# An encoder step on one core: three of the seven products of the FFN's block are accumulated in PSUM onto others

## The chip, the cores and the metric

One core of one Trainium2 chip runs the whole program in one launch. The metric is the device time of one execution in microseconds; the median of the runs shown counts. The core's engines are TensorE (PE, with its weight loader PEld), VectorE (DVE), ScalarE (ACT), GpSimd (POOL) and SyncE (SP, which issues DMAs). Each runs its own queue in order and waits on semaphores for the others.

## The reference

One inference step of an encoder with two layers (DEPTH = 2) and model width 1024, for 512 prompt tokens and 8 x 16 sample tokens. Each layer mixes the tokens by four parallel branches (a gated convolution, two kinds of attention, pooling), and then applies a gated feed-forward network:

```python
h2 = _rmsnorm(x, g_norm[l, 2])
gu = h2 @ w_ffn_in[l]
f = (jax.nn.silu(gu[..., :D_FF]) * gu[..., D_FF:]) @ w_ffn_out[l]
x = x + _rmsnorm(f, g_norm[l, 3])
```

D_FF is 2816. The change lies in the second and third of these lines, in the product with w_ffn_in and what follows it.

## The kernel before

All 640 tokens are treated as one matrix with the model width on the partitions. A product in fp32 is made of three passes: a weight block w is split into a high part whi (a rounded copy, made by ACT at L117) and the rest wlo (a subtraction, by DVE at L274), the tokens likewise into h2's high and low part, and PE adds w-high x x-high, w-high x x-low and w-low x x-high in PSUM.

The FFN's first product is tiled by j = 0 to 21, each j standing for 128 gate and 128 up channels. The first three j (J0 = 3) are done directly. The other 19 are done in `strassen(j)` by a seven-product scheme (Winograd's form of Strassen's): the 1024 x 256 weights of a j are cut into four blocks (upper and lower half of the model width, gate and up), the tokens' matrix into four quadrants (upper and lower half of the width, first and last 320 tokens). Seven products of 512-deep sums replace eight; the price is sums of weight blocks (`weight_sums`, four GpSimd instructions per j, issued for j + 1 in the middle of block j), sums of token quadrants (`token_sums`, made once per layer while the direct j run), and sums of the products.

One product is the function `product(ps, j, p)`: four slices of depth, three passes each, twelve matmuls of 128 x 320 into one PSUM bank. `moving[p]` is the token operand, and `w_sub` hands out the weight block p, split two products ahead. After the second slice, `flush` issues the subtractions wlo that are pending, so that DVE's queue holds, per product, one wlo and then the additions that read the product.

Before the change the seven products of a j go to seven banks: the first to a bank of the pool O, the next two to S, then T, two of D, and S again. The pools hold two D tiles (each of two halves, [128, 2, 512] in fp32), two S, one T and one O, eight banks in all. The order of the products is 0 to 6 in `moving`'s count, and set by `range(7)` in the list of weight chunks. With the products called by Winograd's numbers (p1, p6, p7, p5, p2, p4, p3 in that order), ACT copies p1 to s1, and DVE forms u2 = p6 + s1, u3 = p7 + u2, c22 = p5 + u3, u2 = p5 + u2, s1 = p2 + s1, s1 = u3 - p4, u2 = p3 + u2: seven additions of 128 x 320, each of which reads one bank. ACT applies Silu to s1 (L1868) and, in the next block, to u2 (L1878); DVE multiplies act by s1 and by c22 (L1849, L1881).

All instructions stand in the order in which the code is written; nothing reorders them. In SBUF the results act, X and Y come from a list of 33 slots.

Of the kernel before, what the change touches and what calls it, by code (L numbers as in the profile page):

```python
# [11 lines left out]
AF = mybir.ActivationFunctionType  # L12
ALU = mybir.AluOpType
# [12 lines left out]
HT = T // 2  # L26
# [11 lines left out]
J0 = 3  # L38
GATE_F = 3
GATE_STEP = 0.8  # L40
FO_ORDER = (4, 0, 1, 2, 3, 5, 6, 7, 8, 9, 10)
EPS = 1e-6

# [17 lines left out]
def encoder_step(ctx: ExitStack, tc: tile.TileContext, I, O):  # L61
    nc = tc.nc
    V, A, G, PE, SP = nc.vector, nc.scalar, nc.gpsimd, nc.tensor, nc.sync
# [37 lines left out]
    def psD():  # L101
        return psd.tile([128, 2, 512], F32, tag="D", name=nm("D"))

    def psS():
        return pss.tile([128, 512], F32, tag="S", name=nm("S"))

    def psT():
        return pst.tile([128, 512], F32, tag="T", name=nm("T"))

    def psO():  # L110
        return pso.tile([128, 512], F32, tag="O", name=nm("O"))
# [4 lines left out]
    def copy(out, in_, scale=1.0):  # L116
        A.activation(out=out, in_=in_, func=AF.Copy, scale=scale)  # L117
# [83 lines left out]
    chunks = []  # L201
    for l in range(L):
        for c in ORDER:
            if c == "v":
                chunks += [((k, l, i), I["w_v"][l, g, i], 1032, "n") for g, k in enumerate(("vd", "vf")) for i in range(2)]
            else:
                chunks.append((("in", l, c), I["w_in"][l, c], 1024, "n"))
        for ph, bs in enumerate(PHASES):
            if ph == 2:
                for p in range(5):  # L210
                    for part, f in (((0,), 2 * p - 2), ((1, 2), 2 * p - 1), ((3, 4, 5, 6), -1)):
                        if p < 4:
                            chunks.append((("gs", l, p), None, part, "s"))
                        if f >= 0:
                            chunks.append((("b", l, 2, f), I["w_branch"][l, 1, f, :, 256:512], 256, "n"))
                continue
            for f in range(9):
                for b in bs if f < 8 else bs[:1]:
                    if f < 8:
                        chunks.append((("g", l, ph, b, f), I["w_gate"][l, min(ph, 1), b, f], 1024, "n"))  # L220
                    if b == bs[0] and f > 0:
                        n = 256 * len(bs)
                        chunks.append((("b", l, ph, f - 1), I["w_branch"][l, min(ph, 1), f - 1, :, 256 * bs[0]:256 * bs[0] + n], n, "n"))
        for h, c in ((0, 0), (0, 1), (1, 0), (0, 2), (1, 1), (1, 2), (0, 3), (1, 3)):
            chunks.append((("o", l, h, c), I["w_out"][l, h, c], 1024, "nx"[h]))
        for j in range(NJ):
            if j < J0 or j % 2 == 0:
                for g in range(2):
                    chunks.append((("fi", l, j, g), I["w_fi"][l, j, g], 1024, "n" if j < J0 else "r"))
            if j >= J0:  # L230
                chunks.append((("fs", l, j), None, range(7), "s"))
        for c in FO_ORDER:
            chunks.append((("fo", l, 0, c), I["w_fo"][l, 0, c], 1024, "n"))
        for c in (0, 1, 2, 3, 7, 4, 8, 5, 9, 6, 10):
            chunks.append((("fo", l, 1, c), I["w_fo"][l, 1, c], 1024, "x" if c >= 7 else "n"))
# [172 lines left out]
    def v2(t):  # L408
        return t.rearrange("p (a b) -> p a b", a=2)
# [50 lines left out]
    def quadrant(h, r, c):  # L460
        return [[x[:, 4 * r + k, c * HT:(c + 1) * HT] for k in range(4)] for x in h]

    def token_sums(h, dst, at, step=0.6):
        hv = [f32(x) for x in h]

        def quad(x, r, c, q):
            return hv[x][:, 4 * r + 2 * q:4 * r + 2 * q + 2, c * HT:(c + 1) * HT]

        def chain(E, out, first, terms, q):
            o = v2(out)  # L470
            for n, (x, r, c, op) in enumerate(terms):
                a = o if n else quad(0, *first, q) if isinstance(first, tuple) else v2(first)
                E.tensor_tensor(out=o, in0=a, in1=quad(x, r, c, q), op=op)  # L473

        t = {}
        P_, M_ = ALU.add, ALU.subtract

        def form0(q):
            t[q] = [alloc() for _ in range(4)]
            chain(V, t[q][0], (0, 1), ((0, 0, 0, M_), (1, 0, 1, P_), (1, 0, 0, M_)), q)  # L480
            chain(G, t[q][2], (1, 1), ((0, 0, 1, M_), (1, 1, 1, P_), (1, 0, 1, M_)), q)

        def form1(q):
            o = v2(t[q][1])
            V.tensor_tensor(out=o, in0=quad(0, 1, 1, q), in1=v2(t[q][0]), op=M_)
            V.tensor_tensor(out=o, in0=o, in1=quad(1, 1, 1, q), op=P_)

        def form3(q):
            chain(V, t[q][3], t[q][1], ((0, 1, 0, M_), (1, 1, 0, M_)), q)
            t["formed"] = q  # L490

        def hi(i, q):
            copy(dst(i, q)()[0], t[q][i])

        def lo(i, q):
            d = dst(i, q)()
            sub(d[1], t[q][i], f32(d[0]))
            free(t[q][i])
            t["done"] = t.get("done", 0) + 1

        for q in range(2):
            for fn in (form0, form1, form3):
                after(at, lambda fn=fn, q=q: fn(q))
                at += 2.5 * step
            for i in (1, 0, 2, 3):
                if dst(i, q):
                    after(at, lambda i=i, q=q: hi(i, q))
                    after(at + step, lambda i=i, q=q: lo(i, q))
                    at += step
        return t  # L510
# [490 lines left out]
    def layer(l, Htag, Otag, hT, first_units):  # L1001
# [750 lines left out]
        h2 = (big(Otag + "h"), big(Otag + "l"))  # L1752

        def lhs_o(k, t):
            return tuple(m[:, t * 128:(t + 1) * 128] for m in S.merged[k])

        start = mix_phase(8, lhs_o, "o", range(8), (), range(8), 1, xsrc[2 * l], xsrc[2 * l + 1],
                          {"first": (("fi", l, 0, 0), ("fi", l, 0, 1)), "g": (l, 2), "hi": h2[0], "lo": h2[1]}, lambda n: need(lambda: len(S.merged) > n))
# [50 lines left out]
        tq = (big(Htag + "h"), big(Htag + "l"))  # L1809
        load_blocks(J0)  # L1810
        start(lambda i, Dt: ev_fi(0, i, Dt))
        token_sums(h2, lambda i, q: lambda: [x[:, 2 * i + q, :] for x in tq], 0.0, 0.54)
        for j in range(1, J0):
            for g in range(2):
                Dt = psD()
# [12 lines left out]
        moving = [quadrant(h2, 0, 0), t_op(1), t_op(2), t_op(0), quadrant(h2, 1, 0), t_op(3), quadrant(h2, 1, 1)]  # L1828
        tail = []

        def product(ps, j, p):
            wh, wl = w_sub(("fs", l, j), p)
            xh, xl = moving[p]
            for k in range(4):
                a, b = wh[:, k * 128:(k + 1) * 128], wl[:, k * 128:(k + 1) * 128]
                for pi, (w, x) in enumerate(((a, xh), (a, xl), (b, xh))):
                    PE.matmul(ps[:, :HT], w, x[k], start=(k == 0 and pi == 0), stop=(k == 3 and pi == 2))  # L1837
                if k == 1:
                    flush()
                    tick(1.0)  # L1840
            return ps[:, :HT]

        def strassen(j):
            act, X, Y = alloc(), alloc(), alloc()
            acts[j] = act
            s1, u2, u3, c22 = X[:, :HT], X[:, HT:], Y[:, :HT], Y[:, HT:]

            def add(out, a, b, op=ALU.add):
                V.tensor_tensor(out=out, in0=a, in1=b, op=op)  # L1849

            p1 = product(psO(), j, 0)
            for fn in tail[:1]:
                fn()
            copy(s1, p1)
            p6 = product(psS(), j, 1)
            for fn in tail[1:]:
                fn()
            tail.clear()
            add(u2, p6, s1)
            p7 = product(psS(), j, 2)  # L1860
            add(u3, p7, u2)
            sums(j + 1)
            p5 = product(psT(), j, 3)
            add(c22, p5, u3)
            add(u2, p5, u2)
            p2 = product(psD()[:, 0, :], j, 4)
            add(s1, p2, s1)
            A.activation(out=act[:, :HT], in_=s1, func=AF.Silu)  # L1868
            p4 = product(psD()[:, 0, :], j, 5)
            if j == NJ - 1:  # L1870
                convert(0)
            add(s1, u3, p4, ALU.subtract)
            add(act[:, :HT], act[:, :HT], s1, ALU.mult)
            p3 = product(psS(), j, 6)
            add(u2, p3, u2)

            def gate():
                A.activation(out=act[:, HT:], in_=u2, func=AF.Silu)  # L1878

            def last():  # L1880
                V.tensor_tensor(out=act[:, HT:], in0=act[:, HT:], in1=c22, op=ALU.mult)  # L1881
                free(X, Y)

            tail.extend((gate, last))
# [46 lines left out]
        start = mix_phase(22, lhs_f, "fo", fo_order, range(7), range(14, 22), 3, xsrc[2 * l + 1], O["y"] if last else xsrc[2 * l + 2], nxt, lambda n: convert(n + 1))  # L1931
# [183 lines left out]
```

## Time and profile before

| What | Value |
|---|---|
| Time, median of 3 runs | 2123.02 us (2122.63 to 2124.85) |
| Span of the profiled execution | 2121.1 us |
| Time over that span | 1.9 us, from the median |
| PE busy | 2044.4 us, 96% of the span |
| DVE busy | 1489.7 us, 70% |
| ACT busy | 983.7 us, 46% |
| POOL busy | 694.6 us, 33% |

The times come from runs of their own. The span of the profiled execution reaches from its first to its last instruction; it is the profile's own time, and the durations in the rows below are of that execution. Busy time is an average over stages with different limits, so a stage is read by itself: with the view that sums each engine's busy time in a stretch, and with the waits of that stretch. In a timeline row the first number is the start and the second the duration, in us; what stands in brackets is the engine's idle time before it and what ended it.

### The profile page before, as it was taken

To read this page: it belongs to the slowest core of one execution; us is meant where nothing else is said; L and a number is where in the kernel's file an instruction comes from. 1 tells how busy PE (TensorE), PEld (TensorE's weight loads), DVE (VectorE), ACT (ScalarE), POOL (GpSimd) and SP (SyncE) were. 2 spreads that over 40 slices of the span, in tenths; PEclk is the share of its full clock that TensorE was granted. 3 is DMA by queue.
4 is the path that set the end of the run, shared out by engine and by line. 5 is a ranking of instruction groups with operands and counts; after the bars stand their busy time and mean duration, and the time that the engine had idled before them with its cause. 6 is when DMAs were issued, how large, how long until landed. Compare 5 with 4: busy or idle time off the path is not lost.

```text
span 2121.1 us, 34713 instructions
## 1 busy us (share of the span) xinstructions
PE 2044.4 (96%) x13050; PEld 1927.9 (91%) x13050; DVE 1489.7 (70%) x2746; ACT 983.7 (46%) x2100; POOL 694.6 (33%) x618
## 2 busy tenths in 40 slices
PE   7999999989999999999999999999899999999998
PEld 7999999988889999988899999999888899999887
DVE  5677477689768888853475774775996698888432
ACT  5556455545443433443356554565444444334431
POOL 3111055465315444400040101554751345543000
PEclk9999999999999999999999999999999999999999
DMA  4312244332251222222523122443223422222223
GB/s 146 108 61 86 72 145 138 124 123 75 94 172 60 80 81 91 89 80 75 169 75 117 57 82 82 152 149 130 83 72 115 159 75 80 80 88 67 92 97 119
DMA packets 100744, 214.35 MB, mean 101 GB/s; under 512 B 10896, under 2 KB 35056, under 8 KB 100576
## 3 DMA queue, kind: packets, MB, share of 16 engines
q1 hardware_dynamic: 99552, 209.16, 29.6%
q0 software_dynamic: 1024, 2.98, 0.4%
q8 instruction: 102, 1.67, 0.3%
q14 instruction: 66, 0.54, 0.1%
HBM read 196.02 MB, written 16.08 MB: 100 GB/s over the span
## 4 chain that ended last, share of the span: by engine, by line
PE 68%; DVE 18%; issue 6%; ACT 3%; DMA 2%; POOL 2%; SPq 0%; DVEq 0%; ACTq 0%; POOLq 0%
PE D L376 21%; PE D L1632 11%; PE S L1837 7%; DVE wlo L274 6%; PE D L1837 4%; PE O L1632 3%; PE T L1632 3%; PE D L1413 2%; DVE s L1849 2%; PE T L1837 2%; PE O L1837 2%; PE D L1274 2%; DVE s L473 1%; PE O L808 1%; ACT whi L117 1%
## 5 line engine op out<-in xcount | busy, mean ns | idle before, releaser
L274 DVE TENSOR_TENSOR wlo<-raw,whi 128x512 fp32r<-128x512 f32 (+2 forms) x388 | 294.6, 764 | 183.1 <-ACT whi L117 178.7
L117 ACT ACTIVATE whi<-raw 128x512 fp32r<-128x512 f32 (+2 forms) x390 | 230.3, 606 | 166.9 <-issue 73.8
L274 DVE TENSOR_TENSOR wlo<-s,whi 128x512 fp32r<-128x512 f32 x196 | 210.7, 1077 | 17.9 <-ACT whi L117 16.6
L117 ACT ACTIVATE s<-s 128x512 fp32r<-128x512 f32 (+7 forms) x294 | 176.3, 619 | 91.7 <-POOL s L1425 38.7
L376 PE MATMUL D<-Qh,whi 128*128 128x320 f32 (+2 forms) x736 | 177.1, 315 | 4.0 <-DVE s L1417 3.6
L376 PE MATMUL D<-Ph,whi 128*128 128x320 f32 (+2 forms) x736 | 176.8, 314 | 4.2 <-DVE s L1417 3.5
L338 POOL TENSOR_TENSOR r<-ms,mhalf 128x1 f32<-128x1 f32 x40 | 22.0, 551 | 477.1 <-DVE ms L1677 408.5
L376 PE MATMUL D<-Qh,wlo 128*128 128x320 f32 (+2 forms) x736 | 174.3, 311 | 3.8 <-DVE wlo L274 3.8
L376 PE MATMUL D<-Ph,wlo 128*128 128x320 f32 (+2 forms) x736 | 173.8, 310 | 4.3 <-DVE wlo L274 4.3
L376 PE MATMUL D<-Ql,whi 128*128 128x320 f32 (+2 forms) x736 | 173.8, 310 | 0.0
L376 PE MATMUL D<-Pl,whi 128*128 128x320 f32 (+2 forms) x736 | 173.4, 310 | 0.0
L746 POOL TENSOR_TENSOR s<-s,s 128x512 fp32r<-128x512 f32 x64 | 85.0, 1328 | 181.9 <-ACT s L117 168.9
L117 ACT ACTIVATE whi<-s 128x512 fp32r<-128x512 f32 x196 | 117.3, 621 | 36.4 <-PE S L1837 12.4
L758 POOL TENSOR_TENSOR s<-s,s 128x512 fp32r<-128x512 f32 x64 | 92.9, 1469 | 123.0 <-ACT s L117 100.9
L376 PEld LDWEIGHTS D<-Qh,whi 128*128 128x128 f32 x736 | 123.5, 190 | 6.8 <-DVE s L1417 4.4
L376 PEld LDWEIGHTS D<-Qh,wlo 128*128 128x128 f32 x736 | 125.2, 189 | 4.6 <-DVE wlo L274 4.6
L376 PEld LDWEIGHTS D<-Ph,wlo 128*128 128x128 f32 x736 | 124.5, 189 | 5.3 <-DVE wlo L274 5.3
L376 PEld LDWEIGHTS D<-Ph,whi 128*128 128x128 f32 x736 | 123.0, 189 | 7.0 <-DVE s L1417 4.0
L376 PEld LDWEIGHTS D<-Ql,whi 128*128 128x128 f32 x736 | 125.6, 189 | 0.2
L376 PEld LDWEIGHTS D<-Pl,whi 128*128 128x128 f32 x736 | 125.1, 189 | 0.6 <-DVE Pl L120 0.4
L451 POOL TENSOR_TENSOR s<-V,V 128x512 f32<-128x512 f32 x48 | 77.1, 1607 | 94.4 <-DMA V<-in_w_fi 67.0
L117 ACT ACTIVATE s<-T 128x320 fp32r<-128x320 f32 (+6 forms) x132 | 50.9, 386 | 99.1 <-PE T L520 61.5
(487 smaller groups left out, 5978.9 us busy)
## 6 DMA issues: line engine op xcount, KB each, us to landing
raw<-in_w_gate SPq DMA_DIRECT2D x48, 512.0 KB, 3.5
raw<-in_w_fi SPq DMA_DIRECT2D x48, 512.0 KB, 3.5
raw<-in_w_fo SPq DMA_DIRECT2D x44, 512.0 KB, 3.5
V<-in_w_fi SPq DMA_DIRECT2D x80, 256.0 KB, 3.0
raw<-in_w_in SPq DMA_DIRECT2D x32, 512.0 KB, 3.4
s<-in_ck_d SPq DMA_DIRECT2D x32, 256.0 KB, 4.3
s<-in_cv_d SPq DMA_DIRECT2D x32, 256.0 KB, 4.0
s<-in_ck_f SPq DMA_DIRECT2D x32, 256.0 KB, 4.1
```

Source lines behind the costliest of these rows:

```text
L117: A.activation(out=out, in_=in_, func=AF.Copy, scale=scale)
L274: E.tensor_tensor(out=lo, in0=raw, in1=hi, op=ALU.subtract)
L338: G.tensor_tensor(out=out, in0=ssum, in1=mhalf[:, :n], op=ALU.pow)
L376: PE.matmul(Dt[:, h, :c1 - c0], a, b[:, k, c0:c1], start=(start and pi == 0), stop=(stop and pi == 2))
L451: G.tensor_tensor(out=o[:, :512], in0=x, in1=y, op=op)
L746: G.tensor_tensor(out=lo[:, :512], in0=raw[:, :512], in1=f32(hi[:, :512]), op=ALU.subtract)
L758: G.tensor_tensor(out=lo[:, :512], in0=t[:, :512], in1=f32(hi[:, :512]), op=ALU.subtract)
L1274: PE.matmul(acc[t], x, w[:, kk, :], start=(k == 0 and pi == 0), stop=(k == 7 and pi == 2))
L1413: PE.matmul(Dt[:, h, :HT], w[:, b, k, :], x[:, 2 * br + k, h * HT:(h + 1) * HT], start=(c == 0), stop=(c == 5))
L1632: PE.matmul(ps, a, b, start=(first and pi == 0), stop=(last and pi == 2))
L1837: PE.matmul(ps[:, :HT], w, x[k], start=(k == 0 and pi == 0), stop=(k == 3 and pi == 2))
L1849: V.tensor_tensor(out=out, in0=a, in1=b, op=op)
```

## The change

The three products p2, p7 and p4 no longer get banks of their own: p2 is accumulated onto p1, p7 onto p6, p4 onto p6 + p7, and p3 onto p5. A block uses one S tile (`pa`, for p1 and p2) and one D tile, whose first half (`pb`) holds p6, p7 and p4 and whose second half (`pd`) holds p5 and p3. The order of the products becomes p1, p6, p2, p7, p5, p4, p3 (FS_ORDER). So that p4 may be added, the fourth token sum is formed with the other sign (`negate`). DVE adds five times from PSUM per block: u2 = pb + s1, u3 = pb + s1, c22 = pd + u3, s1 = pb + s1, u2 = pd + u2. The first Silu reads `pa` directly.

```diff
+FS_ORDER = (0, 1, 4, 2, 3, 5, 6)
...
-                chunks.append((("fs", l, j), None, range(7), "s"))
+                chunks.append((("fs", l, j), None, FS_ORDER, "s"))
...
         def form3(q):
-            chain(V, t[q][3], t[q][1], ((0, 1, 0, M_), (1, 1, 0, M_)), q)
+            if negate:
+                o = v2(t[q][3])
+                V.tensor_tensor(out=o, in0=quad(0, 1, 0, q), in1=v2(t[q][1]), op=M_)
+                V.tensor_tensor(out=o, in0=o, in1=quad(1, 1, 0, q), op=P_)
+            else:
+                chain(V, t[q][3], t[q][1], ((0, 1, 0, M_), (1, 1, 0, M_)), q)
...
-        def product(ps, j, p):
+        def product(ps, j, p, more=False):
...
-                    PE.matmul(ps[:, :HT], w, x[k], start=(k == 0 and pi == 0), stop=(k == 3 and pi == 2))
+                    PE.matmul(ps, w, x[k], start=(not more and k == 0 and pi == 0), stop=(k == 3 and pi == 2), skip_group_check=more)
...
-            p1 = product(psO(), j, 0)
+            pa, pbd = psS()[:, :HT], psD()
+            pb, pd = pbd[:, 0, :HT], pbd[:, 1, :HT]
...
+            product(pa, j, 0)
             for fn in tail[:1]:
                 fn()
-            copy(s1, p1)
-            p6 = product(psS(), j, 1)
+            copy(s1, pa)
+            product(pb, j, 1)
             for fn in tail[1:]:
                 fn()
             tail.clear()
-            add(u2, p6, s1)
-            p7 = product(psS(), j, 2)
-            add(u3, p7, u2)
+            add(u2, pb, s1)
+            product(pa, j, 4, True)
+            A.activation(out=act[:, :HT], in_=pa, func=AF.Silu)
             sums(j + 1)
-            p5 = product(psT(), j, 3)
-            add(c22, p5, u3)
-            add(u2, p5, u2)
-            p2 = product(psD()[:, 0, :], j, 4)
-            add(s1, p2, s1)
-            A.activation(out=act[:, :HT], in_=s1, func=AF.Silu)
-            p4 = product(psD()[:, 0, :], j, 5)
+            product(pb, j, 2, True)
+            add(u3, pb, s1)
+            product(pd, j, 3)
+            add(c22, pd, u3)
+            product(pb, j, 5, True)
             if j == NJ - 1:
                 convert(0)
-            add(s1, u3, p4, ALU.subtract)
-            add(act[:, :HT], act[:, :HT], s1, ALU.mult)
-            p3 = product(psS(), j, 6)
-            add(u2, p3, u2)
+            add(s1, pb, s1)
+            V.tensor_tensor(out=act[:, :HT], in0=act[:, :HT], in1=s1, op=ALU.mult)
+            product(pd, j, 6, True)
+            add(u2, pd, u2)
```

How this stands in the queues is shown at two places, both in one block of layer 0. The first is PE's queue, before the change: the matmuls with which the products in places 1 to 5 of a block open, and the third matmul of each, which is the first to use wlo. S, T and D are PSUM tiles, Ph, Pl, Qh and Ql the high and low parts of the tokens, whi and wlo those of the weights; what stands in brackets are the engines' semaphores that the row waits for.

```order
L1837 MATMUL S_8461<-Ph_7540,whi_8422 128x320 [waits Activation_49]
...
L1837 MATMUL S_8461<-Ph_7540,wlo_8423 128x320 [waits DVE_49]
...
L1837 MATMUL S_8480<-Ph_7540,whi_8443 128x320 [waits DVE_49,Activation_49]
...
L1837 MATMUL S_8480<-Ph_7540,wlo_8444 128x320 [waits DVE_49]
...
L1837 MATMUL T_8506<-Ph_7540,whi_8462 128x320 [waits Activation_49]
...
L1837 MATMUL T_8506<-Ph_7540,wlo_8463 128x320 [waits DVE_49]
...
L1837 MATMUL D_8529<-Qh_7011,whi_8481 128x320 [waits Activation_49]
...
L1837 MATMUL D_8529<-Qh_7011,wlo_8482 128x320 [waits DVE_49]
```

The same queue with the change: the opening matmuls of the products in places 2 to 6 and of the next block's first, with the third matmul of places 2 and 4.

```order
L1843 MATMUL S_8421<-Qh_7011,whi_8423 128x320 [waits Activation_49]
...
L1843 MATMUL S_8421<-Qh_7011,wlo_8424 128x320 [waits DVE_49]
...
L1843 MATMUL D_8422<-Ph_7540,whi_8441 128x320 [waits DVE_49,Activation_49]
...
L1843 MATMUL D_8422<-Ph_7540,whi_8459 128x320 [waits DVE_49,Activation_49]
L1843 MATMUL D_8422<-Pl_7541,whi_8459 128x320
L1843 MATMUL D_8422<-Ph_7540,wlo_8460 128x320
...
L1843 MATMUL D_8422<-Ph_7540,whi_8484 128x320 [waits DVE_49,Activation_49]
...
L1843 MATMUL D_8422<-Qh_7011,whi_8505 128x320 [waits DVE_49,Activation_49]
...
L1843 MATMUL S_8560<-Qh_7011,whi_8522 128x320 [waits Activation_49]
```

The wait for DVE has moved from the third matmul to the first in places 3 to 6, and the third no longer has one. The second place is DVE's queue in the same block with the change, from the addition u2 on (s_8419 holds s1 and u2, s_8420 holds u3 and c22, s_8418 is act).

```order
L1856 TENSOR_TENSOR s_8419<-D_8422,s_8419 128x320 [waits PE_49]
L275 TENSOR_TENSOR wlo_8460<-s_8333,whi_8459 128x512 [waits Activation_49]
L275 TENSOR_TENSOR wlo_8485<-raw_8214,whi_8484 128x512 [waits DMAHW6_49,DVE_49,Activation_49]
L1856 TENSOR_TENSOR s_8420<-D_8422,s_8419 128x320 [waits PE_49]
L275 TENSOR_TENSOR wlo_8506<-s_8336,whi_8505 128x512 [waits Activation_49]
L1856 TENSOR_TENSOR s_8420<-D_8422,s_8420 128x320 [waits DVE_49,PE_49]
L275 TENSOR_TENSOR wlo_8523<-V_8351,whi_8522 128x512 [waits DMAHW7_49,Activation_49]
L1856 TENSOR_TENSOR s_8419<-D_8422,s_8419 128x320 [waits PE_49]
L1878 TENSOR_TENSOR s_8418<-s_8418,s_8419 128x320 [waits DVE_49]
L275 TENSOR_TENSOR wlo_8541<-s_8477,whi_8540 128x512 [waits Activation_49]
L1856 TENSOR_TENSOR s_8419<-D_8422,s_8419 128x320 [waits PE_49]
```

All five additions now read the one D tile of the block, one after each of places 1, 3, 4, 5 and 6. The queues of SP and POOL hold the same instructions in the same order as before.

## Rows read from the trace of the kernel before

**Rows 1.** The page, its head and the engines' busy time.
```profile
span 2121.1 us, 34713 instructions
...
PE 2044.4 (96%) x13050; PEld 1927.9 (91%) x13050; DVE 1489.7 (70%) x2746; ACT 983.7 (46%) x2100; POOL 694.6 (33%) x618
```

**Rows 2.** Busy us of PE, PEld, DVE, ACT, POOL; PEclk: both seven-product stages.
```profile
673.25:913.32 240.07, 236.89 (x1599) 233.82 (x1597) 207.69 (x302) 97.61 (x189) 111.65 (x71) 1.00 0.23 79
1722.44:1961.92 239.48, 236.52 (x1598) 233.93 (x1597) 207.12 (x302) 97.57 (x189) 113.05 (x72) 1.00 0.24 79
```

**Rows 3.** Timeline of PE: first matmuls of two neighbouring blocks.
```profile
749.00 0.31 PE L1837 MATMUL O<-Qh,whi 128*128 128x320 f32 x1
...
761.30 0.31 PE L1837 MATMUL O<-Qh,whi 128*128 128x320 f32 x1
```

**Rows 4.** Waits of PEld, total, times, longest: layer 0's stage, then layer 1's.
```profile
PEld S L1837 <- DVE wlo L274: 5.1, 8, 1.0
PEld D L1837 <- DVE wlo L274: 1.2, 4, 0.4
...
PEld S L1837 <- DVE wlo L274: 4.9, 8, 0.7
PEld D L1837 <- DVE wlo L274: 0.7, 2, 0.4
```

**Rows 5.** DVE's groups in layer 0's stage: busy us, mean ns, idle before.
```profile
L1849 DVE TENSOR_TENSOR s<-D,s 128x320 f32<-128x320 f32 x19 | 9.1, 478 | 0.8 <-PE D L1837 0.8
```

**Rows 6.** ACT's groups in the same stretch.
```profile
L117 ACT ACTIVATE whi<-s 128x512 fp32r<-128x512 f32 x74 | 44.4, 622 | 17.9 <-PE S L1837 7.9 <-POOL s L451 6.0 <-DVE s L1881 2.2
...
L1868 ACT ACTIVATE s<-s 128x320 f32<-128x320 f32 x19 | 9.0, 472 | 71.9 <-DVE s L1849 71.9
```

**Rows 7.** Timeline of all engines: DVE waits for the product in T.
```profile
680.13 0.31 PE L1837 MATMUL T<-Ph,wlo 128*128 128x320 f32 x1
...
680.28 0.31 PE L1837 MATMUL D<-Qh,whi 128*128 128x320 f32 x1
...
680.48 0.89 DVE L1849 TENSOR_TENSOR s<-T,s 128x320 f32<-128x320 f32 x2 [0.67 <-PE T L1837]
```

**Rows 8.** Timeline of DVE, then of PE: PE waits for wlo and restarts.
```profile
787.74 1.78 DVE L274 TENSOR_TENSOR wlo<-s,whi 128x512 fp32r<-128x512 f32 x1
...
789.57 0.41 PE L1837 MATMUL S<-Ph,wlo 128*128 128x320 f32 x1 [0.59 <-DVE wlo L274]
789.82 0.31 PE L1837 MATMUL S<-Ph,whi 128*128 128x320 f32 x1
```

**Rows 9.** Timelines of PE, ACT and DVE in the block from 749.00.
```profile
750.62 0.31 PE L1837 MATMUL O<-Qh,wlo 128*128 128x320 f32 x1
...
750.96 0.44 ACT L117 ACTIVATE s<-O 128x320 f32<-128x320 f32 x1 [0.58 <-PE O L1837]
...
752.81 1.58 DVE L1881 TENSOR_TENSOR s<-s,s 128x320 f32<-128x320 f32 x1
754.31 0.48 DVE L1849 TENSOR_TENSOR s<-S,s 128x320 f32<-128x320 f32 x1
...
756.42 0.67 DVE L274 TENSOR_TENSOR wlo<-V,whi 128x512 fp32r<-128x512 f32 x1
```

**Rows 10.** Timelines of PE around two longer stops, before the stage and in an earlier one.
```profile
654.63 0.56 PE L376 MATMUL D<-Qh,wlo 128*128 128x320 f32 x2 [2.23 <-DVE wlo L274]
...
656.05 0.73 PE L376 MATMUL D<-Qh,whi 128*128 128x320 f32 x2
...
659.20 0.46 PE L376 MATMUL D<-Qh,whi 128*128 128x320 f32 x2
...
387.11 0.56 PE L376 MATMUL D<-Ph,whi 128*128 128x320 f32 x2 [2.24 <-DVE s L1417]
387.51 0.45 PE L376 MATMUL D<-Pl,whi 128*128 128x320 f32 x2
387.80 0.45 PE L376 MATMUL D<-Ph,wlo 128*128 128x320 f32 x2
```

More of the change, by code (lines that the diff above doesn't have):

```diff
@@ L461, in quadrant, with token_sums @@
         return [[x[:, 4 * r + k, c * HT:(c + 1) * HT] for k in range(4)] for x in h]
-    def token_sums(h, dst, at, step=0.6):
+    def token_sums(h, dst, at, step=0.6, negate=False):
         hv = [f32(x) for x in h]
@@ L1811, in layer @@
         start(lambda i, Dt: ev_fi(0, i, Dt))
-        token_sums(h2, lambda i, q: lambda: [x[:, 2 * i + q, :] for x in tq], 0.0, 0.54)
+        token_sums(h2, lambda i, q: lambda: [x[:, 2 * i + q, :] for x in tq], 0.0, 0.54, True)
         for j in range(1, J0):
@@ L1840, in product @@
                     tick(1.0)
-            return ps[:, :HT]
         def strassen(j):
@@ L1846, in strassen, with add @@
             s1, u2, u3, c22 = X[:, :HT], X[:, HT:], Y[:, :HT], Y[:, HT:]
-            def add(out, a, b, op=ALU.add):
-                V.tensor_tensor(out=out, in0=a, in1=b, op=op)
-            p1 = product(psO(), j, 0)
+            pa, pbd = psS()[:, :HT], psD()
+            pb, pd = pbd[:, 0, :HT], pbd[:, 1, :HT]
+            def add(out, a, b):
+                V.tensor_tensor(out=out, in0=a, in1=b, op=ALU.add)
+            product(pa, j, 0)
             for fn in tail[:1]:
                 fn()
-            copy(s1, p1)
-            p6 = product(psS(), j, 1)
+            copy(s1, pa)
+            product(pb, j, 1)
             for fn in tail[1:]:
```

## The prediction, made blind

> **What bounds the kernel now.** I read the page first, then cut out the two stages that the change touches, then TensorE's (PE's) waits in them, then single rows. PE is busy for 96% of the span and VectorE (DVE) for 70% [rows 1]. The seven-product stage runs once per layer; cut from its first matmul to the first matmul behind it, it lasts 240.07 and 239.48 us, 479.55 us in all, and PE is busy nearly throughout at the full clock [rows 2]. There are 19 blocks in a layer, 38 in all. A block in which PE never waits goes from 749.00 to 761.30, 12.30 us for 84 matmuls of 128x320, 0.146 us each and 1.76 us for a product of twelve [rows 3]. So 38 x 12.30 = 467.4 us of the 479.55 us is plain matmul work that the change leaves alone, and **12.1 us** is all that the stage could win from fewer waits. What PE waits for there is always the same thing: the low half of a weight block (wlo) that DVE has not finished; the weight loader's waits are 5.1 + 1.2 us and 4.9 + 0.7 us [rows 4], which is 11.9 us and accounts for them. DVE is late because it is the fullest engine beside PE (207.69 us of 240.07 in the first stage [rows 2]).
>
> **What the change removes.** Two of seven DVE additions from PSUM leave each block. One takes 478 ns [rows 5], so DVE loses 38 x 2 x 0.48 = 36.5 us of work. Off the path that is worth nothing by itself; on the path it can at most remove PE's 12.1 us of waits. I take all of it, **-12.1 us**, because the new waits below also give DVE more time in each block (bounds: 0 and -12.1). The first Silu now reads the bank straight from ScalarE. It waited 71.9 us per layer for a DVE addition [rows 6], but nothing on PE's path hung on it except the weight copies queued behind it, and they end in the same 12.1 us. The negated sum in token_sums is two subtractions and additions for two subtractions: zero. GpSimd's and SyncE's queues keep their rows in the same order, and the block's weights are still released by the product in place 5, so no DMA moves past another; the one weight block that moves (a12, from place 4 to place 2) was loaded together with the one for place 0.
>
> **What the change adds.** PE now writes banks that DVE or ScalarE still has to read, and each such write waits. Call the seven products of a block places 0 to 6. The order rows show what waits. Before, almost every product opened with a wait for ScalarE and its third matmul waited for DVE's wlo. Now the products in places 3, 4, 5 and 6 open with a wait for DVE, and their third matmul waits for nothing, so the count awaited at the front already covers wlo. For place 4 this fixes which DVE instruction it is: on DVE the rows run u2, wlo for place 4, wlo for place 5, u3; a wait that covers wlo and belongs to the D tile can only be u3. But place 4 opens the other half of D, which nothing has read. D is one tile with two halves, and the program guards it as a whole. The awaited counts in the built program say the same for all three: place 4 waits for u3 (which reads place 3's result), place 5 for c22 (place 4's), place 6 for the sum for the gate (place 5's). **Each of these three additions cannot begin before the product just ahead has ended, so PE has nothing to do meanwhile.** Places 2 and 3 wait too, but with a whole product between.
>
> The price of one wait without slack, from rows:
> - The last matmul of T starts at 680.13 and DVE, idle and waiting for it, starts its addition at 680.48: 0.35 us [rows 7].
> - The addition takes 0.48 us [rows 5].
> - From DVE's end to the matmul that waited: 787.74 + 1.78 = 789.52, matmul at 789.57, 0.05 us [rows 8]. The weight load waits there as well, as it does here.
> - The step from that matmul to the next is 789.82 - 789.57 = 0.25 us [rows 8] where 0.146 is usual: 0.10 us.
> - Without a wait the next matmul would have come 0.15 us after the last one.
>
> 0.35 + 0.48 + 0.05 + 0.10 - 0.15 = **0.83 us**; three per block and 38 blocks: **+94.6 us**. The low bound drops the way back and the refill: 0.68 us, +77.5 us. The high bound puts one wlo of 0.67 us [rows 9] ahead of one of the three additions in each block: +120 us. I take the middle sum, since by the order the wlo ahead of c22 and of the gate's sum has its copy long done, and the one ahead of u3 ends about when place 3 does: Silu starts 0.34 us after place 2's last matmul (the copy from O) [rows 9], takes 0.47, the copy of whi 0.62, wlo 0.67 [rows 6, 9]; together 2.1 us, against 1.76 + 0.35 us until u3 could start anyway.
>
> The waits with slack. Place 2 waits for ScalarE's copy of place 0's bank; that copy starts 0.34 us after the last matmul of O and takes 0.44 [rows 9], and place 1 covers it with 1.76 us: zero. Place 3 waits for u2, which reads place 1. Before, in the block that starts at 749.00, that addition ran at 754.31 [rows 9] and ended at 754.79, 0.5 us after place 3's start (749.00 + 3 x 1.76 = 754.28), because GpSimd's weight sums run beside DVE: a wlo takes 0.67 us without and up to 1.78 us with them, a 128x320 product from SBUF up to 1.58 us [rows 8, 9]. So 0 to 0.65 us per block. Now GpSimd's sums will start earlier in the block, since their DMA is released by place 5's wlo, which comes earlier, and each block is 2.5 us longer; most of the overlap falls on places 5 and 6. I take 0.2 us: **+7.6 us** (bounds 0 and +25).
>
> The sum: -12.1 + 94.6 + 7.6 = **+90.1 us**. The profiled span of 2121.1 us becomes 2211.2 us. The median of the runs shown is 2123.02 us, 1.9 us over that span, and I keep those 1.9 us: **2213 us**, 4.2% slower. What PE does in a block is then 12.30 + 2.5 + 0.2 = 15.0 us.
>
> The Trainium skill says otherwise of the wait in place 4: "PSUM — Partial Sum Buffer", section "Summary: rules for kernel authors", tells to read PSUM beside a running matmul from a different bank, and to guard by bank. The two halves of D are 512 fp32 each, one bank each by that page, so the chip would need no wait there; by that rule the sum would be that of the first rival. The trace agrees for two tiles (DVE reads T from 680.48 on while PE writes D [rows 7]) and shows nothing for two halves of one. The order rows show the wait built in all the same.
>
> **The rivals.**
> 1. *Faster: the three waits cost nothing*, because what they await is done by the time PE comes, the halves of D being as free of each other as T and D are now, where DVE reads T while PE writes D [rows 7]. Place: the opening matmuls of places 4 to 6. Price: only the -12.1 us remain, 2123.0 - 12.1 = 2111 us. It decides if the counts point at additions one product further back. Against it stands the order argument above. Chance 0.04.
> 2. *DVE is late as well*: GpSimd's sums stay beside places 1 to 3 as now, u2 comes 0.65 us late in each block and one wlo of 0.67 us stands ahead of u3: 38 x 1.32 = 50.2 us in place of the 7.6: 2256 us. For it: today's block at 749.00. Against it: DVE has 2 x 0.48 us less to do in a block that is 2.5 us longer. Chance 0.10.
> 3. *The clock falls too.* After PE stood still for 2.23 us before 654.63, six pairs of matmuls from 656.05 to 659.20 came 0.53 us apart on average, which is the 1.2 GHz level; after a stop of 2.24 us before 387.11 pairs came 0.29 us apart (387.51 to 387.80), the 2.4 GHz level [rows 10]. The new stops are 0.7 us long, three in each block, and stops of 0.6 us in the stage leave the granted clock at 1.00 [rows 2, 8]. Six pairs at 0.53 - 0.29 cost 1.4 us; once in each block 38 x 1.4 = 53 us: 2266 us. Chance 0.04. The Trainium skill, "TensorE: Matmul & The Clock Gate", section "A second HAM failure mode: psum-queue depth-cycling", tells of a kernel whose short PE stops between groups of matmuls made the clock swing; no run so far shows that for stops as short as these.
> 4. *No change*: the waits cost about what the removed stalls give, 0.1 us each (38 x 3 x 0.1 = 11.4 us). That needs DVE's addition to overlap the product that it reads, which no row shows. Chance 0.01.
>
> **How the numbers follow.** The forecast has 0.81 and its own range is 2188 (three waits at 0.68 us, nothing else: 2123 - 12.1 + 77.5 = 2188.4) to 2238 (2123 - 12.1 + 120 + 7.6 = 2238.5). The range reaches on to 2246 for a part of rival 2. A measurement can tell 0.2%, 4 us. Faster is rival 1, 0.04; within 0.2% is rival 4, 0.01; slower is the rest, 0.95.
>
> **What would show it right or wrong.** In the changed kernel PE's waits in the two stages must be for DVE's additions at L1856, three per block, some 0.7 us each, ahead of products that write D; the waits for wlo must be gone or nearly; a stage must last about 285 us; DVE's busy time in the stage must fall to about 190 us; the granted clock must stay at 1.00. I am wrong if those products start without a gap (rival 1), if gaps ahead of place 3 are as large as those ahead of 4 to 6 (rival 2), or if matmuls in the stage come 0.29 us apart singly (rival 3).

## The result, and the profile after

The changed kernel takes **2213.45 us** (median of five) against 2123.39 us: ratio 1.0428, 95% interval 1.041 to 1.0445, so 90 us or 4.3% slower. One execution of the five was disturbed from end to end (9019 us); the other four lie between 2211.09 and 2220.09 us, with a median of 2212.32 us. The profile below is of the same kernel run once more (2211.51 us).

The head of the page, which answers to [rows 1]:

```profile
span 2209.7 us, 34693 instructions
...
PE 2065.0 (93%) x13050; PEld 1928.5 (87%) x13050; DVE 1446.6 (65%) x2670; ACT 988.3 (45%) x2100; POOL 676.5 (31%) x618
```

DVE has 76 instructions fewer, two per block. Its busy time falls by 1489.7 - 1446.6 = 43.1 us, and yet the span grows by 88.6 us. Where, the busy time by stretch tells; the two stages again, in the columns of [rows 2]:

```profile
671.46:957.08 285.62, 247.14 (x1598) 233.91 (x1597) 186.78 (x266) 99.83 (x189) 102.29 (x71) 1.00 0.20 66
1764.79:2050.57 285.78, 247.31 (x1599) 233.95 (x1598) 186.78 (x266) 99.89 (x189) 102.09 (x71) 1.00 0.20 66
```

The stages last 571.40 us where they lasted 479.55 [rows 2]: 91.85 us more, all of the difference and a little over. The granted clock is still 1.00. PE's waits in the first stage (total, times, longest):

```profile
PE D L1843 <- DVE s L1856: 26.3, 39, 0.7
PE D L1843 <- ACT whi L118: 12.2, 18, 0.7
```

These are 57 waits, three for each of 19 blocks; none for wlo is left of those in [rows 4]. The second row, with a weight copy of ACT (L118) as what ended the wait, is a mislabel, as the timelines of DVE, ACT and PE for one block show:

```profile
708.76 0.49 DVE L1856 TENSOR_TENSOR s<-D,s 128x320 f32<-128x320 f32 x1
...
711.41 0.49 DVE L1856 TENSOR_TENSOR s<-D,s 128x320 f32<-128x320 f32 x1 [1.56 <-PE D L1843]
...
707.33 0.62 ACT L118 ACTIVATE whi<-V 128x512 fp32r<-128x512 f32 x1
...
711.31 0.63 ACT L118 ACTIVATE whi<-s 128x512 fp32r<-128x512 f32 x1 [2.07 <-PE D L1843]
...
708.41 0.31 PE L1843 MATMUL D<-Ph,wlo 128*128 128x320 f32 x1
709.40 0.38 PE L1843 MATMUL D<-Ph,whi 128*128 128x320 f32 x1 [0.68 <-DVE s L1856]
709.62 0.31 PE L1843 MATMUL D<-Pl,whi 128*128 128x320 f32 x1
...
712.05 0.38 PE L1843 MATMUL D<-Ph,whi 128*128 128x320 f32 x1 [0.68 <-ACT whi L118]
...
714.72 0.38 PE L1843 MATMUL D<-Qh,whi 128*128 128x320 f32 x1 [0.68 <-DVE s L1856]
```

Place 3 ends with the matmul of 708.41; u3 runs from 708.76 to 709.25; place 4 starts at 709.40. Places 5 and 6 follow at 712.05 and 714.72, each behind a gap of the same length. Of place 5's two candidates, the copy that ended last before it (from 711.31 to 711.94) belongs to the next block by the order of the copies; place 5's own copy is that of 707.33, done by 707.95, four microseconds before 712.05. What place 5 came 0.15 us after is DVE's c22, which ended at 711.90. The wait that ends last is DVE's addition in all three; the run with half additions, below, settles it for place 5.

### The profile page after: what moved, and what is told of

Its sections match the earlier page's. It is cut to its first block, busy times and chain, and to the rows that moved or that the text cites. A ratio compares the mean times of both kernels' runs of the same rounds, so it can differ in the third digit from the quotient of the medians.

```text
span 9017.4 us, 34693 instructions
## 1 busy us (share of the span) xinstructions
PE 8924.0 (99%) x13050; PEld 7562.2 (84%) x13050; DVE 1313.4 (15%) x2670; ACT 997.4 (11%) x2100; POOL 618.3 (7%) x618
## 4 chain that ended last, share of the span: by engine, by line
PE 99%; DVE 1%; issue 0%; DMA 0%; SPq 0%; DVEq 0%; POOLq 0%; ACT 0%; ACTq 0%
PE D L377 33%; PE D L1843 17%; PE D L1638 11%; PE S L1843 7%; PE D L1419 6%; PE T L1638 4%; PE O L1638 4%; PE S L1543 2%; PE O L814 2%; PE D L1280 2%; PE D L1543 1%; PE S L879 1%; PE S L362 1%; PE T L526 1%; PE S L928 1%; PE O L718 1%
## 5 line engine op out<-in xcount | busy, mean ns | idle before, releaser
L377 PE MATMUL D<-Ph,whi 128*128 128x320 f32 (+2 forms) x736 | 728.6, 1159 | 0.0
L377 PE MATMUL D<-Ph,wlo 128*128 128x320 f32 (+2 forms) x736 | 721.5, 1145 | 0.0
L377 PE MATMUL D<-Pl,whi 128*128 128x320 f32 (+2 forms) x736 | 720.3, 1144 | 0.0
L377 PEld LDWEIGHTS D<-Ph,wlo 128*128 128x128 f32 x736 | 603.8, 861 | 10.3 <-issue 6.3
L377 PEld LDWEIGHTS D<-Pl,whi 128*128 128x128 f32 x736 | 603.3, 855 | 10.4 <-issue 6.4
L377 PEld LDWEIGHTS D<-Ph,whi 128*128 128x128 f32 x736 | 586.9, 851 | 24.1 <-issue 19.7
L377 PE MATMUL D<-Qh,wlo 128*128 128x320 f32 (+2 forms) x736 | 525.9, 843 | 0.0
L1843 PE MATMUL D<-Ph,whi 128*128 128x320 f32 x380 | 427.6, 1125 | 38.5 <-DVE s L1856 38.5
L1843 PE MATMUL D<-Ph,wlo 128*128 128x320 f32 x380 | 426.6, 1123 | 0.0
L1843 PE MATMUL D<-Pl,whi 128*128 128x320 f32 x380 | 419.9, 1105 | 0.0
L118 ACT ACTIVATE whi<-raw 128x512 fp32r<-128x512 f32 (+2 forms) x390 | 232.7, 606 | 1376.7 <-issue 497.5
L1843 PEld LDWEIGHTS D<-Ph,whi 128*128 128x128 f32 x380 | 293.1, 771 | 99.1 <-ACT whi L118 89.8
L1843 PE MATMUL D<-Qh,whi 128*128 128x320 f32 x380 | 333.8, 878 | 38.5 <-DVE s L1856 38.5
L1843 PEld LDWEIGHTS D<-Pl,whi 128*128 128x128 f32 x380 | 320.0, 842 | 2.5
```

Source lines behind the costliest of these rows:

```text
L377: PE.matmul(Dt[:, h, :c1 - c0], a, b[:, k, c0:c1], start=(start and pi == 0), stop=(stop and pi == 2))
L1843: PE.matmul(ps, w, x[k], start=(not more and k == 0 and pi == 0), stop=(k == 3 and pi == 2), skip_group_check=more)
```

## The experiments

Each run is compared with runs of the kernel before on the same chip, median 2123.56 us (2123.57 us for the last four). "Place" counts the products of a block in their order of execution, 0 to 6.

**The changed kernel, for its profile** (no edit).

> The changed kernel, unaltered, for an undisturbed profile. Theory (three waits without slack per block): time 2205 to 2220 us; in the two stages PE's waits for DVE's additions at L1856 come to about 38 x 3 x 0.7 = 80 us, three per block, each stage lasts about 285 us, and hardly any wait for wlo is left. Rival (DVE is late instead): gaps ahead of place 3 as large as those ahead of places 4 to 6.

2211.51 us, one run. Three waits per block, stages of 285.62 and 285.78 us, no wait ahead of place 3: the theory's signs, and not the rival's.

**pd in a tile of its own.**

```diff
-            pb, pd = pbd[:, 0, :HT], pbd[:, 1, :HT]
+            pb, pd = pbd[:, 0, :HT], psT()[:, :HT]
```

> One part undone: pd, the bank of p5 and p3, is a T tile of its own instead of the second half of D; same products, same order, same five additions. Theory (the loss is the guard on D as a whole): all three waits without slack go, 38 x 3 x 0.83 = 94.6 us, and the time comes to 2111 to 2125 us, at or a little under the kernel before. Rival (the loss comes from the order of the products or from DVE being late): the time stays above 2190 us.

2126.45 us, ratio 1.0007 (0.9992 to 1.0022). The order of the products, the five additions and all accumulation are as in the changed kernel; only the guard differs, and 85 of the 2211.51 us are gone. The loss is the guard on D as one tile, not the order and not DVE's work. (The order rows of the change show that guard as a semaphore wait of the program; what the chip would do with two halves that are not guarded as one, no run shows.) But the kernel does not come under the kernel before, and the time is 1.5 us over the theory's range. Its stages, and PE's waits in the first of them:

```profile
672.67:914.23 241.56, 237.16 (x1599) 233.92 (x1597) 197.59 (x266) 98.86 (x189) 110.32 (x71) 1.00 0.24 78
1723.48:1964.78 241.30, 236.96 (x1599) 233.93 (x1598) 197.96 (x266) 98.83 (x189) 111.20 (x72) 1.00 0.23 79
```
```profile
PE D L1843 <- ACT s L1868: 2.2, 4, 0.6
PE D L1843 <- DVE s L1856: 2.0, 4, 0.8
```

482.86 us, 3.3 us more than before, with DVE 9 to 10 us less busy in each. The 57 waits of the changed kernel's stage are down to 8, and they have moved: the timelines of POOL, DVE and PE in one block show place 3's, which must wait for u2.

```profile
749.58 1.74 POOL L452 TENSOR_TENSOR s<-raw,raw 128x512 f32<-128x512 f32 x1
751.28 1.74 POOL L452 TENSOR_TENSOR s<-raw,s 128x512 f32<-128x512 f32 x1
...
751.95 1.62 DVE L275 TENSOR_TENSOR wlo<-s,whi 128x512 fp32r<-128x512 f32 x1
753.49 0.48 DVE L1886 TENSOR_TENSOR s<-s,s 128x320 f32<-128x320 f32 x1
753.89 0.48 DVE L1856 TENSOR_TENSOR s<-D,s 128x320 f32<-128x320 f32 x1
...
754.51 0.39 PE L1843 MATMUL D<-Ph,whi 128*128 128x320 f32 x1 [0.54 <-ACT s L1868]
```

u2 (753.89) stands behind a wlo that took 1.62 us beside GpSimd's sums and behind the last multiplication of the block before. (The wait's label names Silu, and PE starts 0.14 us after u2's end at 754.37, as it does after the other additions.)

**One wait in place of three.**

```diff
-            product(pb, j, 5, True)
+            pt = psT()[:, :HT]
+            product(pt, j, 5)
...
-            add(s1, pb, s1)
+            add(s1, pt, u3)
```

> One wait in place of three: p4 goes to a T tile of its own and is added to u3, so places 5 and 6 write nothing that was read just before, while place 4 still opens the second half of D behind u3. Theory (0.83 us for each wait, additive): two waits less, 2213 - 2 x 38 x 0.83 = 2150 us, 2140 to 2158. Rival (one wait makes the others cheaper or dearer, or the cost is not per wait): outside that; with the cost in the order alone, above 2190 us.

2149.81 us, ratio 1.0113 (1.0081 to 1.0145), where 2150 was expected. In the first stage PE's waits for DVE are one per block, and each is as long as in the changed kernel (12.8 / 19 = 0.67 us idle, 38.5 / 57 = 0.68 us there): the cost is per wait and adds up.

```profile
PE D L1843 <- DVE s L1856: 12.8, 19, 0.7
```
```profile
670.08:923.62 253.54, 240.07 (x1599) 233.79 (x1597) 190.76 (x266) 98.90 (x189) 111.19 (x71) 1.00 0.23 74
1731.34:1985.00 253.66, 240.11 (x1599) 233.85 (x1597) 190.95 (x266) 98.79 (x189) 111.98 (x72) 1.00 0.23 75
```

That the time fell on 2150 is in part luck. A wait costs 0.91 us and not 0.83 (see the next section), so two fewer save 69 us and not 63. But of the 253.54 + 253.66 = 507.20 us the floor of 467.50 us (found below) and 38 waits of 0.91 us leave 5 us. They stand ahead of place 3, which waits for u2 here too: in 8 of the 19 blocks of each stage it opens about 0.38 us after the last matmul where 0.15 is usual. A matmul's row is 0.31 us long, so the view of waits does not list this. One such block:

```profile
754.86 0.48 DVE L1856 TENSOR_TENSOR s<-D,s 128x320 f32<-128x320 f32 x1
...
755.10 0.31 PE L1843 MATMUL S<-Qh,wlo 128*128 128x320 f32 x1
755.48 0.39 PE L1843 MATMUL D<-Ph,whi 128*128 128x320 f32 x1
```

**p2 alone: the kernel before with one of the accumulations.** (The change has four of them, p2, p7, p4 and p3; the title counts three.)

```diff
-                chunks.append((("fs", l, j), None, range(7), "s"))
+                chunks.append((("fs", l, j), None, FS_ORDER, "s"))
...
-            p1 = product(psO(), j, 0)
+            pa = psO()
+            p1 = product(pa, j, 0)
...
+            p12 = product(pa, j, 4, True)
+            A.activation(out=act[:, :HT], in_=p12, func=AF.Silu)
+            sums(j + 1)
             p7 = product(psS(), j, 2)
             add(u3, p7, u2)
-            sums(j + 1)
...
-            p2 = product(psD()[:, 0, :], j, 4)
-            add(s1, p2, s1)
-            A.activation(out=act[:, :HT], in_=s1, func=AF.Silu)
```

> The kernel before with one part of the change alone: p2 goes to place 2 and is accumulated onto p1, Silu reads that bank, six additions instead of seven; the other products keep their banks. Theory (a fewer addition is worth only what PE waits for wlo, 12.1 us in all): 2111 to 2124 us. Rival (the order of the products costs by itself): over 2130 us.

2107.87 us, ratio 0.9914 (0.9886 to 0.9942): faster than the kernel before, and 3 us under the theory's range. Its stages have practically no wait left:

```profile
670.81:904.87 234.06, 233.97 (x1598) 233.65 (x1597) 206.85 (x285) 99.01 (x189) 111.63 (x72) 1.00 0.25 81
1711.25:1945.13 233.88, 233.88 (x1599) 233.88 (x1597) 205.12 (x285) 98.89 (x189) 111.70 (x72) 1.00 0.24 81
```

467.94 us, 11.6 us under [rows 2], as expected. DVE is nearly as busy as before (206.85 against 207.69 us), so what helped is not the load but the order: the Silu that reads its bank directly no longer stands on ACT for a DVE addition (71.9 us in the first stage [rows 6]) with the weight copies behind it. DVE's waits for those copies, before and with p2 alone, bear that out:

```profile
DVE wlo L274 <- ACT whi L117: 27.6, 30, 1.1
```
```profile
DVE wlo L275 <- ACT whi L118: 6.9, 9, 1.6
```

That this is all of it is argued from the queue; the run changed the addition and the order together.

**p2 alone again**, beside the runs that follow.

> The same kernel as in the run with p2 alone, beside these runs, to compare it with five additions on one chip and to see whether its gain over the kernel before is the 11.6 us that the two stages show or more. Theory: 2104 to 2114 us. Rival (a disturbance of that run): nearer to 2120 us.

2109.28 us, ratio 0.9931 (0.9913 to 0.9949). The gain stands. The two runs are 14 to 16 us under the kernel before, of which the stages show 11.6; where the other 3 or 4 us are, outside the stages, is not settled. The profiled executions of these two runs, one and the same kernel, differ there by 4 us themselves (2104.3 - 467.94 = 1636.4 and 2108.2 - 467.91 = 1640.3).

**p7 in a bank of its own: five additions, and no write right behind a read.**

```diff
-            pa, pbd = psS()[:, :HT], psD()
-            pb, pd = pbd[:, 0, :HT], pbd[:, 1, :HT]
+            pa, p6, pb, pd = (f()[:, :HT] for f in (psO, psS, psS, psT))
...
-            product(pb, j, 1)
+            product(p6, j, 1)
...
-            add(u2, pb, s1)
+            add(u2, p6, s1)
...
-            product(pb, j, 2, True)
-            add(u3, pb, s1)
+            product(pb, j, 2)
+            add(u3, pb, u2)
...
-            add(s1, pb, s1)
+            add(s1, pb, u2)
```

> Five additions, and no write right behind a read: pd in a tile of its own, and also p7 opens a bank of its own (p2 onto p1, p4 onto p7, p3 onto p5), so place 3 no longer waits for u2. Theory (what is left over the floor in the run with pd in its own tile is place 3's wait for u2, about 7.4 us per layer): the two stages come to their floor of 234 us each without a wait, and the time to that of the run with p2 alone, 2104 to 2112 us; the sixth addition fewer brings nothing more. Rival (fewer additions pay by themselves): under 2102 us. Rival (accumulating costs in itself): over 2116 us.

2112.78 us, ratio 0.9949 (0.9933 to 0.9966), 0.8 us over the range expected.

```profile
673.33:906.95 233.62, 233.62 (x1598) 233.62 (x1597) 195.79 (x266) 98.90 (x189) 110.53 (x71) 1.00 0.23 81
1719.03:1952.91 233.88, 233.88 (x1599) 233.88 (x1598) 196.55 (x266) 98.83 (x189) 111.59 (x72) 1.00 0.23 81
```

PE is busy for the whole of both stages. So place 3's wait was what stood over the floor, the floor of the two stages is 467.50 us, and accumulating costs PE nothing in itself. With 9 to 11 us less of DVE's work per stage than the run with p2 alone it is not faster: at the floor, one addition fewer buys nothing.

**u2 ahead of the last multiplication of the block before**, in the run with pd in its own tile.

```diff
+            add(u2, pb, s1)
             for fn in tail[1:]:
                 fn()
             tail.clear()
-            add(u2, pb, s1)
```

> The run with pd in its own tile, with one instruction moved on DVE: u2 is issued ahead of the last multiplication of the block before (L1886) instead of behind it. Theory (u2 is late because DVE is late at the start of a block, beside GpSimd's sums): u2 comes 0.4 us or more earlier, place 3's waits of 14.7 us in both layers fall under 5 us, and the time comes to 2109 to 2118 us. Rival (place 3 waits for something else, ScalarE or its own weights): the waits stay at 12 us or more and the time at 2122 us or more.

2121.57 us, ratio 0.9993 (0.9983 to 1.0003): neither.

```profile
674.13:913.21 239.08, 236.59 (x1598) 233.83 (x1597) 199.22 (x266) 98.86 (x189) 111.11 (x71) 1.00 0.23 79
1722.22:1960.70 238.48, 236.20 (x1598) 233.89 (x1597) 197.56 (x266) 98.82 (x189) 115.00 (x72) 1.00 0.23 80
```

477.56 us, 5.3 us less than with u2 behind, but 10.1 us over the floor, 8.6 of them ahead of place 3 by the starts of PE's matmuls, where under 5 was expected. The direction is the theory's; the size is not. In the timelines of DVE, ACT and PE u2 still stands behind two subtractions beside GpSimd's sums:

```profile
751.03 1.38 DVE L275 TENSOR_TENSOR wlo<-V,whi 128x512 fp32r<-128x512 f32 x1
752.49 1.62 DVE L275 TENSOR_TENSOR wlo<-s,whi 128x512 fp32r<-128x512 f32 x1
754.04 0.48 DVE L1856 TENSOR_TENSOR s<-D,s 128x320 f32<-128x320 f32 x1
...
754.45 0.44 ACT L1868 ACTIVATE s<-S 128x320 f32<-128x320 f32 x1 [1.48 <-PE S L1843]
...
754.66 0.39 PE L1843 MATMUL D<-Ph,whi 128*128 128x320 f32 x1 [0.25 <-DVE s L1856]
```

Place 3 opens 0.14 us after u2's end and while the Silu still runs (to 754.89), so it is u2 that it waits for, and not the Silu, which the label named in the run with u2 behind. That GpSimd is the cause of the subtractions' length was not tried by itself.

**Half additions.** The three awaited additions, and the multiplication that reads c22, in the changed kernel:

```diff
-            add(u3, pb, s1)
+            add(u3[:, :160], pb[:, :160], s1[:, :160])
...
-            add(c22, pd, u3)
+            add(c22[:, :160], pd[:, :160], u3[:, :160])
...
-            add(s1, pb, s1)
+            add(s1[:, :160], pb[:, :160], s1[:, :160])
...
-                V.tensor_tensor(out=act[:, HT:], in0=act[:, HT:], in1=c22, op=ALU.mult)
+                V.tensor_tensor(out=act[:, HT:HT + 160], in0=act[:, HT:HT + 160], in1=c22[:, :160], op=ALU.mult)
```

> The changed kernel with the three awaited additions (u3, c22, the gate's sum) and the multiplication that reads c22 cut to 160 of 320 columns; half of these sums is left out. Theory (each wait holds the whole addition, so it shrinks with it): each of the 114 waits becomes 0.15 to 0.18 us shorter, 17 to 21 us in all, 2190 to 2196 us. Rival (the price is the handshake between the engines alone): 2208 us or more.

2196.80 us, ratio 1.0348 (1.0328 to 1.0369); 0.8 us over the range, far from the rival (2208 or more). The group of the shortened additions (minimum, median, maximum in ns) and the stages:

```profile
L1856 DVE TENSOR_TENSOR s<-D,s x190: 324/325/492, 678.0 to 2035.8; 128x160 f32<-128x160 f32 x114, 128x320 f32<-128x320 f32 x76
```
```profile
674.33:950.46 276.13, 247.14 (x1598) 233.91 (x1597) 178.25 (x266) 100.59 (x189) 105.99 (x71) 1.00 0.20 68
1759.48:2035.61 276.13, 247.15 (x1598) 233.89 (x1597) 178.45 (x266) 100.55 (x189) 106.05 (x71) 1.00 0.20 68
```

The stages are 571.40 - 552.26 = 19.1 us shorter, 0.168 us for each of 114 waits; the addition is 0.49 - 0.325 = 0.165 us shorter. The whole addition lies in the wait. DVE, ACT and PE at place 5 of one block:

```profile
713.13 0.33 DVE L1856 TENSOR_TENSOR s<-D,s 128x160 f32<-128x160 f32 x1 [1.58 <-PE D L1843]
...
713.04 0.63 ACT L118 ACTIVATE whi<-s 128x512 fp32r<-128x512 f32 x1 [1.93 <-PE D L1843]
...
713.61 0.38 PE L1843 MATMUL D<-Ph,whi 128*128 128x320 f32 x1 [0.51 <-DVE s L1856]
```

Place 5 starts 0.15 us after the shortened c22 (713.46) and before that copy of ACT's ends (713.67), so it does not wait for the copy.

## Why the prediction was right

It gave 2213 us, and the mechanism that it named is the one that the runs show; that it came so near is luck in part. By its own steps:

- **The three waits without slack** are there, at places 4, 5 and 6, in every block, and the guard on D as a whole makes them (pd in its own tile). Their price was a little low. Over the floor of 467.50 us the changed kernel's stages have 571.40 - 467.50 = 103.9 us, 0.91 us for each of 114 waits where the sum had 0.83. In the block shown the pieces are 0.35 us from the last matmul to u3, 0.49 for u3, **0.15** from its end to the matmul that waited, and 0.22 - 0.15 = 0.07 for the next step, less the usual 0.15: 0.91. The way back was taken as 0.05 us from a wait for wlo [rows 8], and measured 0.15. There the wait stands at a product's third matmul; here it stands ahead of the whole product. The term should have been 103.9 us instead of 94.6.
- **The removed waits**: all 12.1 us were taken as gone, and no wait for wlo is left. Measured against the floor, before had 479.55 - 467.50 = 12.05 us. The reason given for them, that DVE is the fullest engine beside PE, does not hold: with p2 alone DVE is as busy and the waits are gone. Of the two routes that the prediction saw, DVE's work and the weight copies behind the Silu, the runs favour the second.
- **Place 3's wait for u2** was put at 7.6 us and is zero. The longer block did even more than the prediction said: GpSimd's sums fall on places 4 to 6 and the start of the next block, so DVE is on time for u2. In the block of the timeline above, GpSimd's first and last sum, then u2, which ends at 705.97, and the opening of place 3 0.83 us later, with no gap ahead of it:

```profile
711.40 1.28 POOL L452 TENSOR_TENSOR s<-V,V 128x512 f32<-128x512 f32 x1 [8.23 <-DMA V<-in_w_fi]
...
715.57 1.54 POOL L452 TENSOR_TENSOR s<-V,s 128x512 f32<-128x512 f32 x1
...
705.49 0.48 DVE L1856 TENSOR_TENSOR s<-D,s 128x320 f32<-128x320 f32 x1
...
706.80 0.31 PE L1843 MATMUL D<-Ph,whi 128*128 128x320 f32 x1
```

  With one of the three waits left some 5 us of it are back, and in the run with pd in its own tile, whose blocks are short again, 482.86 - 467.50 = 15.4 us. It is the prediction's second rival in small, hidden in the changed kernel by the three larger waits.
- So the forecast sits 0.5 us from the median by errors that cancel: 9.3 us too little for the waits, 7.6 us too much for u2. And the stages grew by 91.85 us where the span grew by 88.6: some 3 us went elsewhere, which no step foresaw and which is within what one kernel's executions differ by outside the stages.
- **Rival 1** (faster, the waits cost nothing) falls with the timeline above. The rule of the Trainium skill behind it, from "PSUM — Partial Sum Buffer", section "Summary: rules for kernel authors", is not contradicted: with p5 and p3 in another tile, DVE reads one bank while PE writes another and the loss is gone. The built program was guarded more widely than the rule asks.
- **Rival 3** (the clock falls): the granted clock is 1.00 in both stages, with 114 stops of 0.68 us on average and none over 0.7. The depth-cycling that the Trainium skill's "TensorE: Matmul & The Clock Gate" describes, section "A second HAM failure mode: psum-queue depth-cycling", does not show here.
- **Rival 4** (no change) falls with the price of a wait.

One signpost was rough: DVE's busy time in a stage was put at about 190 us and is 186.78. The block's 15.0 us are right (285.62 / 19 = 15.03).

## What to carry to other kernels

Accumulating a product onto a bank that another engine still reads turns its evacuation into a wait, and what matters is how many products stand between the read and the next write: with none the wait cost 0.91 us each time, with one it was free or cost some tenths. Look also at what the program guards: two halves of one PSUM tile were guarded as one, and a tile of its own for the second half gave back 85 us. Count a saved instruction by the wait that it shortens: here 12 us was all there was in the stages, the first accumulation took it, with the earlier Silu that came with it (2107.87 us, the fastest version tried), and the second saved addition brought nothing more.

## What the runs showed of the hardware that was not expected

- The way from DVE's last write to the first matmul of a product that waited for it took 0.15 us in all 114 waits (0.145 to 0.147), against 0.055 to 0.057 us in the 22 waits for wlo in the middle of a product that the kernel before has in its stages. Why the two differ is open.
- PE's row can name the wrong releaser when a product waits for two engines: 18 of the 57 waits in a stage were put down to a weight copy that belongs to the next block and ended some 0.1 us before, just behind the addition that was awaited.
- PE needs no more time for a matmul that adds onto a product that has been read in between: the stages with five additions run at the same 467.5 us floor as those with six, and as 38 blocks of 12.30 us would [rows 3].
- DVE's additions that read a bank (128x320, one input in PSUM and one in SBUF) kept their length beside GpSimd's sums, while the gate's multiplication of the same size, with both inputs in SBUF, did not. In the stages of the kernel before, 54 of the 114 additions from S ran beside those sums and took at most 0.49 us, as the other 60 did; the multiplication took 1.07 to 1.41 us beside them (16 times) and 0.49 without (22 times).

```profile
L1849 DVE TENSOR_TENSOR s<-S,s x114: 475/478/492, 677.0 to 1963.1; 128x320 f32<-128x320 f32 x114
L1849 DVE TENSOR_TENSOR s<-s,s x38: 491/493/1408, 685.1 to 1962.0; 128x320 f32<-128x320 f32 x38
```
